# Output projection of the pooling chunks as seven products of quartered matrices, with the sums of quarters made two stages earlier and kept in DRAM

## Chip, cores, metric

The kernel runs on one core of a Trainium2 chip. The metric is the device time of one execution in microseconds, the median of several runs. TensorE (PE) multiplies, VectorE (DVE), ScalarE (ACT) and GpSimd (POOL) do the elementwise work, and SyncE (SP) issues most of the DMAs.

## What is computed

One layer of a streaming encoder on x of 1024 rows by 1024 columns, in float32:

```python
h = rmsnorm(x, norm1_g)
proj = h @ w_in                      # q, k, v (512 each), 8 forget logits, u (512)
attn = forgetting_attention(q, k, v, log_f)       # 8 heads of 64, causal
pool = multiscale_pool(u, w_pool, pool_scale)     # 4 groups of 128 channels
mixed = concat([attn, pool])         # 1024 rows x 1024
x = x + mixed @ w_out                # the output projection
h2 = rmsnorm(x, norm2_g)
x = x + (silu(h2 @ w_gate) * (h2 @ w_up)) @ w_down
y = rmsnorm(x, final_g)
```

The change concerns the line `x + mixed @ w_out`. Its contraction of 1024 is cut into eight chunks of 128: chunks 0 to 3 are the four pairs of attention heads, chunks 4 to 7 the four pooling groups.

## The kernel before

Every large product is made in three matmuls of a reduced-precision type. `split` (L119) copies a page to a high part on ACT (L120) and subtracts it from the page on DVE or POOL for a low part (L121). `mm3` (L159) multiplies high by high, high by low and low by high (L161 to L163).

The input projection and the pooling groups come first; the four pooled chunks are stored to the DRAM tensor `mixd`. Then `attend` (L711) runs four times, once for each pair of heads. A pair has eight jobs (two heads by four blocks of 256 rows). A job's steps are the turning of probabilities (`turn`, L634), the products with the values (`values`, L651, into the single bank `po`), `combine` (L662), which stores the attention rows to `mixd` through SP, and the `scores` (L605) of the next job: matmuls, a masked minimum on DVE, an exponential on ACT, a reciprocal on DVE and a normalisation on POOL (L629). Scores run one job ahead (`LOOK = 1`).

Between these steps `attend` takes matmuls from a generator, the filler; `counts` says how many filler steps each job is given. For the first three pairs the filler is the projection of the next pair's q and k (`project`, L533), and the values of the last two pairs (`project_v23`, L580). The order of the trace of the program gives priorities; a planner then fixes each engine's order by its own estimate of when operands are ready, so a filler matmul may come earlier than its place in the text. On each engine, and in the DMA queue of SP, the order is then fixed.

In the last pair the filler is the first part of the output projection. `first_rows` (L817) multiplies chunks 4 and 5 for the eight row tiles, `second_rows` (L844) chunks 6, 7 and 0. A row tile has two halves of 512 columns; each half is one accumulation in one of the two PSUM banks with the tag "m" (`rows2`, L803), then a DVE add into the row of x2 in SBUF (L811). There are 32 filler steps; 27 are given to the jobs, one is taken behind them, and four are held behind the last product with the values (`mark["pv"]`, L897). Then `last_row` (L873) adds chunks 1, 2 and 3 to each row, stores it and goes on to the second norm and the gate and up projections. The chunk of the last pair, mix 3, comes back from DRAM in two halves (`mix_halves`, L859).

A page of 128 by 1024 is loaded by `raw_page` (L750) into a raw tile and split by `split_page` (L756). Raw tiles have the tag "wr" with two buffers, which also holds the raw weights and the low half of the keys in `project`; some raw pages are loaded to tiles of the pool `outp`, which opens with `xw` (the rows of x2) when the transposed input `hTh`, `hTl` is freed behind the last projection. `first_chunk` (L763) splits chunk 4 during the third pair. The buffer "vc" of `vpool` holds `pf01` at first, and then the values of the third pair.

Of the kernel before, what the change touches and what calls it, by code (L numbers as in the profile page):

```python
# [8 lines left out]
F32 = mybir.dt.float32  # L9
# [6 lines left out]
P = 128  # L16
S = 1024
# [28 lines left out]
def tile_kernel(  # L46
# [664 lines left out]
    def attend(p, fill, counts, drain=True):  # L711
# [7 lines left out]
        for n in range(2 * NSB):  # L719
            steps = job_steps(2 * NSB * p + n)  # L720
# [23 lines left out]
    attend(0, project(1), [5, 4, 4, 3, 8, 6, 6, 0])  # L744
    attend(1, both(project(2), project_v23()), [10, 7, 6, 8, 10, 8, 12, 0])
    W, VB, VC = (wpool,), (vpool, ("vb",), 1), (vpool, ("vc",), 1)
    ST0, ST1 = (ap_, ("st0", "st0"), 6), (ap_, ("st1", "st1"), 6)
    raw_pages = {}

    def raw_page(kind, c, pl, tag):  # L750

        t = raw_pages[kind, c] = pl.tile([P, 1024], F32, tag=tag, bufs=2, name=f"r_{kind}{c}")
        row = (PAIR[c] if c < NPAIR else c) * P
        nc.sync.dma_start(out=t, in_=mixd[c] if kind == "mix" else w_out[0, row : row + P, :])

    def split_page(kind, c, to, eng):  # L756
        pages = page_tiles(to, f"{kind}{c}")
        split(*pages, raw_pages.pop((kind, c)), eng)
        return pages

    ahead = {}

    def first_chunk():  # L763

        for kind, to in (("mix", VB), ("wo", W)):
            raw_page(kind, NPAIR, wpool, "wr")
            ahead[kind] = [split_page(kind, NPAIR, to, nc.gpsimd)]
        raw_page("mix", NPAIR + 1, wpool, "wr")
# [46 lines left out]
    last = {}  # L815

    def first_rows():  # L817

        raw_page("wo", 5, op, "ol")
        x2_load(ORDER[0])  # L820
        lhs, rhs = ahead["mix"], ahead["wo"]
        lhs.append(split_page("mix", 5, M, nc.vector))
        rhs.append(split_page("wo", 5, O, nc.vector))
        x2_load(ORDER[1])
        for kind, c, tag in (("wo", 6, "oh"), ("mix", 6, "ml"), ("wo", 7, "mh"), ("mix", 7, "ol")):
            raw_page(kind, c, op, tag)
        later = [
            ("wo", 6, VC, nc.vector), ("mix", 6, ST0, nc.gpsimd), ("wo", 7, W, nc.vector),
            ("mix", 7, ST1, nc.gpsimd), ("wo", 0, ST0, nc.vector), ("mix", 0, VB, nc.gpsimd),
        ]  # L830
        for n, tt in enumerate(ORDER):
            if n + 2 < NT:
                x2_load(ORDER[n + 2])
            if n == 2:
                raw_page("wo", 0, wpool, "wr")
# [594 lines left out]
```

## Time and profile before

| | before |
|---|---|
| median of 3 runs | 1035.35 us (1035.22 to 1036.37) |
| profiled execution: span from first to last instruction | 1033.6 us |
| profiled execution: its own time | given by its span alone |
| PE, DVE, ACT, POOL busy | 1024.3, 632.8, 454.2, 381.1 us |
| mean granted TensorE clock | 0.998 |
| HBM read, written | 86.29 MB, 33.03 MB |

The profile is one execution. Busy time is the time in which at least one instruction of the engine was recorded; matmuls are pipelined, so a record of a matmul is longer than the distance to the next. A releaser behind an idle time is the operation that ended it, inferred from semaphores. A window row gives a stretch, then for PE, weight loads, DVE, ACT and POOL the busy time and the number of instructions, then the granted clock, the share of the DMA engines and GB/s; for one tile it lists only the engines that touch the tile.

### The profile page before, as it was taken

To read this page: it belongs to the slowest core of one execution; us is meant where nothing else is said; L and a number is where in the kernel's file an instruction comes from. 1 tells how busy PE (TensorE), PEld (TensorE's weight loads), DVE (VectorE), ACT (ScalarE), POOL (GpSimd) and SP (SyncE) were. 2 spreads that over 40 slices of the span, in tenths; PEclk is the share of its full clock that TensorE was granted. 3 is DMA by queue.
4 is the path that set the end of the run, shared out by engine and by line. 5 is a ranking of instruction groups with operands and counts; after the bars stand their busy time and mean duration, and the time that the engine had idled before them with its cause. 6 is when DMAs were issued, how large, how long until landed. Compare 5 with 4: busy or idle time off the path is not lost.

```text
span 1033.6 us, 14202 instructions
## 1 busy us (share of the span) xinstructions
PE 1024.3 (99%) x5104; PEld 868.9 (84%) x5104; DVE 632.8 (61%) x1000; ACT 454.2 (44%) x733; POOL 381.1 (37%) x312
## 2 busy tenths in 40 slices
PE   9999999999999999999999999999999999999997
PEld 7988888998888888888888888888888888888886
DVE  7565566776886479744433334334334789788886
ACT  7434355665665257533333233233233343333346
POOL 4350121213346043447537536636637510000045
PEclk9999999999999999999999999999999999999999
DMA  7224434333643134343143143143236755353424
GB/s 251 53 47 143 105 81 103 84 102 89 224 175 106 49 136 129 103 143 112 62 132 113 62 133 112 64 131 113 81 113 251 248 204 175 110 198 97 153 92 163
DMA packets 108439, 130.21 MB, mean 126 GB/s; under 512 B 7369, under 2 KB 70353, under 8 KB 108369
## 3 DMA queue, kind: packets, MB, share of 16 engines
q1 hardware_dynamic: 96544, 108.18, 33.4%
q10 hardware_dynamic: 11504, 20.47, 5.2%
q8 instruction: 40, 0.66, 0.2%
q0 software_dynamic: 320, 0.66, 0.2%
q14 instruction: 31, 0.25, 0.1%
HBM read 86.29 MB, written 33.03 MB: 115 GB/s over the span
## 4 chain that ended last, share of the span: by engine, by line
PE 98%; DMA 1%; ACT 0%; DVE 0%; POOL 0%; issue 0%; ACTq 0%; POOLq 0%
PE gu_P L161 14%; PE gu_P L162 14%; PE gu_P L163 14%; PE d L161 7%; PE d L162 7%; PE d L163 7%; PE po L657 4%; PE tp L643 3%; PE o L161 3%; PE o L162 3%; PE qk L161 3%; PE qk L162 3%; PE qk L163 3%; PE o L163 3%; PE v L374 2%; PE z L618 2%
## 5 line engine op out<-in xcount | busy, mean ns | idle before, releaser
L121 DVE TENSOR_TENSOR gu_P_l<-s,gu_P_h 128x1024 fp32r<-128x1024 f32 (+1 forms) x48 | 66.5, 1393 | 98.6 <-ACT gu_P_h L120 98.5
L162 PE MATMUL d<-d,d 128*128 128x512 f32 (+1 forms) x308 | 119.5, 388 | 0.0
L163 PE MATMUL d<-d,d 128*128 128x512 f32 (+1 forms) x308 | 119.5, 388 | 0.0
L629 POOL TENSOR_SCALAR p<-p,rr 128x128 f32<-128x128 f32 (+3 forms) x64 | 48.6, 764 | 175.5 <-DVE rr L628 140.2
L161 PE MATMUL d<-d,d 128*128 128x512 f32 x308 | 107.8, 388 | 0.0
L120 ACT ACTIVATE d<-r_f 128x1536 fp32r<-128x1536 f32 (+1 forms) x28 | 38.8, 1384 | 117.6 <-PE d L162 101.6
L121 DVE TENSOR_TENSOR gu_P_l<-r,gu_P_h 128x1024 fp32r<-128x1024 f32 x32 | 48.9, 1527 | 64.3 <-ACT gu_P_h L120 64.3
L1063 POOL TENSOR_TENSOR s<-r 128x1024 f32<-128x1024 f32 x10 | 24.0, 2401 | 161.9 <-DMA r<-in_w_up_dram 116.0
L120 ACT ACTIVATE gu_P_h<-r 128x1024 fp32r<-128x1024 f32 x32 | 33.8, 1060 | 91.1 <-PE gu_P L162 35.5
L162 PEld LDWEIGHTS d<-d,d 128*128 128x128 f32 x308 | 57.8, 188 | 12.0 <-DVE d L121 0.2
L161 PEld LDWEIGHTS d<-d,d 128*128 128x128 f32 x308 | 57.8, 188 | 12.0
L163 PEld LDWEIGHTS d<-d,d 128*128 128x128 f32 x308 | 57.8, 188 | 11.9
L626 ACT ACTIVATE p<-p,mn 128x128 f32<-128x128 f32 (+3 forms) x64 | 49.3, 772 | 32.8 <-DVE mn L620 29.9
L1291 POOL TENSOR_SCALAR sse<-sse 128x1 f32<-128x1 f32 x7 | 3.5, 494 | 158.1 <-ACT junk L1287 158.1
L1150 POOL TENSOR_TENSOR h<-h,qh 128x512 f32<-128x512 f32 x33 | 44.3, 1345 | 32.3 <-ACT qh L1148 24.1
L648 DVE TENSOR_TENSOR tl<-tp,th 128x512 fp32r<-128x512 f32 (+1 forms) x80 | 49.3, 632 | 10.7 <-ACT th L647 9.7
L120 ACT ACTIVATE gu_P_h<-s 128x1024 fp32r<-128x1024 f32 (+1 forms) x48 | 47.0, 984 | 19.7 <-PE gu_P L162 13.0
L1147 DVE TENSOR_TENSOR qh<-gu_P,sn_sU 128x512 f32<-128x512 f32 x22 | 15.2, 690 | 60.5 <-POOL h L1150 43.2
L121 DVE TENSOR_TENSOR d<-r_f,d 128x1536 fp32r<-128x1536 f32 (+1 forms) x28 | 45.7, 1633 | 10.5 <-ACT d L120 10.5
L163 PE MATMUL qk<-hTh,l_qk 128*128 128x512 f32 x128 | 50.7, 396 | 0.0
L161 PE MATMUL qk<-hTh,h_qk 128*128 128x512 f32 x128 | 50.6, 395 | 0.0
L162 PE MATMUL qk<-hTl,h_qk 128*128 128x512 f32 x128 | 50.4, 394 | 0.0
(337 smaller groups left out, 3067.1 us busy)
## 6 DMA issues: line engine op xcount, KB each, us to landing
r_f<-hsdP SPq DMA_DIRECT2D x77, 256.0 KB
r_wd<-in_w_down_dram SPq DMA_DIRECT2D x22, 512.0 KB
hsdP<-f ACTq DMA_DIRECT2D x43, 256.0 KB
r<-in_w_gate_dram SPq DMA_DIRECT2D x21, 512.0 KB
r<-in_w_up_dram SPq DMA_DIRECT2D x21, 512.0 KB
s<-hi SPq DMA_DIRECT2D x64, 128.0 KB
hsdP<-h ACTq DMA_DIRECT2D x32, 256.0 KB
x<-in_x_dram SPq DMA_DIRECT2D x8, 512.0 KB
```

Of the source, the lines that this page charges most:

```text
L120: mark["hi"] = nc.scalar.activation(out=hi, in_=src, func=AF.Copy)
L121: return eng.tensor_tensor(out=lo, in0=src, in1=f32(hi), op=ALU.subtract)
L161: nc.tensor.matmul(ps, lh, rh, start=start, stop=False, **kw)
L162: nc.tensor.matmul(ps, lh, rl, start=False, stop=False, **kw)
L163: mark["mm"] = nc.tensor.matmul(ps, ll, rh, start=False, stop=stop, **kw)
L626: nc.scalar.activation(out=pr[:, :n], in_=pr[:, :n], func=AF.Exp, scale=-1.0, bias=mn, accum_out=rs)
L629: nc.gpsimd.tensor_scalar(out=pr[:, :n], in0=pr[:, :n], scalar1=rr, scalar2=1.0, op0=ALU.mult, op1=ALU.mult)
L643: nc.tensor.transpose(tp[:, w : w + P], probs[h, 2 * sb + a][:, s * P : (s + 1) * P], ident)
L648: nc.vector.tensor_tensor(out=tl[:, :w], in0=tp[:, :w], in1=f32(th[:, :w]), op=ALU.subtract)
L657: mark["pv"] = nc.tensor.matmul(po[:, first * P : 2 * P], vt[p][:, s, j, :], part[:, o : o + wd], start=(s == 0 and part is th), stop=(s = ...
L1063: g(out=s1, in0=a21, in1=a22, op=ALU.add)
L1150: nc.gpsimd.tensor_tensor(out=h, in0=h, in1=q, op=ALU.mult)
```

## The change

The four pooling chunks are taken as one product of a 1024 x 512 matrix by a 512 x 1024 matrix, cut into quarters of 512 x 256 and 256 x 512, and computed by the Winograd form of Strassen's method: seven products of quarters in place of eight, and eight sums of quarters, four for each side.

- `quarter_load`, `quarter_sums` and `quarter_store` make these sums in four rounds during the first two pairs of heads. A round loads four half pages (two DMAs of 512 KB) into one tile of 1 MB with the tag "vc", makes four sums in place on POOL and stores the tile to a DRAM tensor `sumd`. The twelve parts are put in at the beginnings of jobs by the new argument `events`.
- `raw_page` loads an operand of a product in two halves of 256 KB, from `mixd` and `w_out` or from `sumd`, always into a "wr" tile. `SPLITS` lists the pages with the engine of the low part and the filler step before which each is put; each loads the page two places on.
- The filler is one generator, `output_steps`, of 32 steps. P6 goes to four halves of two new tiles `total` (an ACT copy). P7 is added to x2, and its bank is then continued with P4. P1 is added to the totals, and POOL adds them to x2; its bank is continued with P2 and chunk 0. P5 is added to the totals, which POOL adds to two places of x2. P3 takes chunk 0 in the same bank. The last four steps, `rest`, are chunk 0 for the remaining eight half rows, one bank for each three matmuls.
- The loads of the eight rows of x2, put in one for each row before, are all put in ahead of the last pair.
- Chunks 1, 2 and 3 are split as before, through the list, and multiplied in `last_row` as before.

The core of the diff:

```diff
+    def quarter_load(r):
+        kind, i = rounds[r]
+        t = quarters[r] = vpool.tile([P, 4, 512], F32, tag="vc", bufs=1, name=f"quarters{r}")
+        for k in range(2):
+            dst = t[:, 2 * k : 2 * k + 2, :].rearrange("p a e -> p (a e)")
+            nc.sync.dma_start(out=dst, in_=page_source(kind, NPAIR + 2 * k + i))
...
+        if rounds[r][0] == "mix":
+            go(q3, q1, q3, ALU.add)
+            go(q1, q0, q1)
+            go(q0, q3, q0)
+            go(q2, q2, q0)
...
+    def quarter_store(r):
+        nc.sync.dma_start(out=sumd[rounds[r]], in_=quarters[r])
...
+    attend(0, project(1), [5, 4, 4, 3, 8, 6, 6, 0], events={n: side(n) for n in range(8)})
+    attend(
+        1, both(project(2), project_v23()), [10, 7, 6, 8, 10, 8, 12, 0], events={n: side(8 + n) for n in range(4)}
+    )
...
+        t = raw_pages[kind, c] = wpool.tile([P, 1024], F32, tag="wr", bufs=2, name=f"r_{kind}{c}")
...
+    def add_total(c, *places):
+        for tt, hf in places:
+            out = x2_half(tt, hf)
+            nc.gpsimd.tensor_tensor(out=out, in0=out, in1=total_of(c), op=ALU.add)
+
+    def part(ps, k, c, start, stop):
+        (ah, al), (bh, bl) = operands["mix", k], operands["wo", k]
+        for i in range(2):
+            ts, hs = slice(i * 512 + c * P, i * 512 + (c + 1) * P), slice(i * 512, (i + 1) * 512)
+            mm3(ps, ah[:, ts], al[:, ts], bh[:, hs], bl[:, hs], start and i == 0, stop and i == 1, True)
...
+    SPLITS = [
+        ("mix", "P7", M, nc.vector, -1), ("wo", "P7", O, nc.vector, 0),
+        ("mix", "P4", M, nc.vector, 2), ("wo", "P4", O, nc.vector, 3),
+        ("mix", "P1", VB, nc.gpsimd, 4), ("wo", "P1", W, nc.gpsimd, 5), ("wo", "P2", W, nc.gpsimd, 6),
+        ("mix", 0, VC, nc.gpsimd, 7), ("wo", 0, ST1, nc.vector, 8), ("mix", "P2", O, nc.vector, 11),
+        ("mix", "P5", M, nc.gpsimd, 12), ("wo", "P5", O, nc.gpsimd, 13), ("wo", 1, M, nc.gpsimd, 14),
+        ("mix", "P3", VB, nc.vector, 19), ("wo", "P3", W, nc.vector, 20), ("wo", 3, W, nc.gpsimd, 21),
+        ("mix", 1, O, nc.gpsimd, 22), ("mix", 2, M, nc.gpsimd, 25), ("wo", 2, O, nc.gpsimd, 26),
+    ]
...
+        order = [(p6, c) for c in range(NH)] + pairs(p7, p4) + pairs(p1, p2)
+        order += [(f, c) for f in (p5, p3, rest) for c in range(NH)]
+        for s, (f, c) in enumerate(order):
+            ahead_of(s)
+            f(c)
+            yield
+
+    raw_page(*SPLITS[1][:2])
+    ahead_of(-1)
+    for tt in (*range(NH, NT), *range(NH)):
+        x2_load(tt)
+    fill = output_steps()
     attend(3, fill, [3, 3, 4, 4, 4, 4, 3, 2], drain=False)
```

More of the change, by code (lines that the diff above doesn't have):

```diff
@@ L747, in tile_kernel @@
     ST0, ST1 = (ap_, ("st0", "st0"), 6), (ap_, ("st1", "st1"), 6)
[L748 to L754, printed above, removed]
+    raw_pages, operands = {}, {}
+    QUARTER = dict(
+        mix=dict(P1=(0, 0), P2=(1, 0), P4=(1, 1), P6=0, P7=1, P3=2, P5=3),
+        wo=dict(P1=(0, 0), P2=(1, 0), P3=(1, 1), P5=0, P7=1, P4=2, P6=3),
+    )
@@ L842, in tile_kernel @@
[L842 to L853 removed]
+    total = [ap_.tile([P, S], F32, tag="st0", bufs=6, name=f"total{n}") for n in range(2)]
```

137 lines of the change are left out of this document (94 added, 43 removed).

## The prediction

> **What bounds the kernel now.** I read the first part of the page, then the chain that ended last, then the waits of PE, then the busy times of the one stage that the change rebuilds.
>
> ```profile
> span 1033.6 us, 14202 instructions
> PE 1024.3 (99%) x5104; PEld 868.9 (84%) x5104; DVE 632.8 (61%) x1000; ACT 454.2 (44%) x733; POOL 381.1 (37%) x312
> PE 98%; DMA 1%; ACT 0%; DVE 0%; POOL 0%; issue 0%; ACTq 0%; POOLq 0%
> ...
> 264.80:349.80 85.00, 85.00 (x506) 74.97 (x505) 64.44 (x156) 48.88 (x94) 34.86 (x27) 1.00 0.45 154
> 349.80:358.20 8.40, 8.40 (x40) 6.98 (x39) 3.71 (x6) 1.64 (x3) 0.00 (x0) 1.00 0.24 73
> ...
> PE warm L254 <- DVE junk L252: 1.2, 1, 1.2
> ...
> PE spread L264 <- DVE gcol L260: 0.3, 1, 0.3
> ```
>
> TensorE is busy in 99% of the span and is 98% of the chain. Its listed waits are four, of 2.5 us in sum, all in the opening. The two window rows are the last pair of heads (264.8 to 349.8 us), where the first part of the output projection is the filler between attention steps, and the stretch after the last attention product. Columns: length, PE, PEld, DVE, ACT, POOL busy, granted clock, DMA share, GB/s. PE has no gap in either, DVE is busy for 64.44 of 85.00 us. So a product taken away is worth its PE time, as long as the rest of the filler is ready when PE wants it.
>
> **The change, part by part.**
>
> *Products removed.* Before, the filler is 16 output blocks (8 row tiles by 2 halves) of five chunks, three matmuls each: 240. After it is seven products of 4 row tiles, 2 contraction halves and 3 matmuls (168) plus chunk 0 for 16 blocks (48): 216. The last three chunks stay. So 24 matmuls go. Their price is not the 0.39 us of a record, since they are pipelined, but the distance between starts:
>
> ```profile
> 350.25 0.39 PE L162 MATMUL o<-hl_wo,h_mix 128*128 128x512 f32 x1
> ...
> 357.99 0.39 PE L163 MATMUL o<-h_wo,hl_mix 128*128 128x512 f32 x1
> 358.21 0.39 PE L161 MATMUL o<-h_wo,h_mix 128*128 128x512 f32 x1
> ...
> 349.97:358.21 8.24, 8.24 (x36) 6.81 (x37) 2.06 (x3) 1.00 0.25 75
> 358.41 0.69 DVE L811 TENSOR_TENSOR x_s<-o,x_s 128x512 f32<-128x512 f32 x1 [0.63 <-PE o L163]
> ```
>
> The last row of the window counts 36 from 349.97, so 35 from 350.25 to 358.21: 7.96 / 35 = 0.2274 us. 24 x 0.2274 = 5.46 us, 0.53% of the span. Twelve of them leave the stage with attention (204 to 192), twelve the tail behind the last attention product (36 to 24).
>
> *The last four steps are two-bank bound.* Each of the eight last blocks ("rest") has three matmuls in one of two banks, then a DVE add. Above, the third matmul starts at 357.99 and its add ends at 358.41 + 0.69 = 359.10, 1.11 us later. A bank is then busy 2 x 0.2274 + 1.11 = 1.56 us, and with 0.05 us for PE to restart 1.61; PE needs 6 x 0.2274 = 1.36 for two blocks. Lost: 0.25 us per pair, four pairs: **+1.0 us**. Below: 0, if something else fills. Above: two splits of mix chunk 3 push in front of the adds:
>
> ```profile
> 353.84 0.69 DVE L121 TENSOR_TENSOR mix_l<-r_mix,mix_h 128x512 fp32r<-128x512 f32 x1 [0.86 <-ACT mix_h L120]
> 356.49 0.69 DVE L121 TENSOR_TENSOR mix_l<-r_mix,mix_h 128x512 fp32r<-128x512 f32 x1 [1.35 <-ACT mix_h L120]
> 359.57 0.39 PE L161 MATMUL o<-h_wo,mix_h 128*128 128x512 f32 x1
> ```
>
> 2 x 0.6 more makes 2.2 us. The tail also covers the trip of mix chunk 3 through DRAM: its first half is ready at 354.53, wanted at 359.57, and with 12 x 0.2274 = 2.7 us less at 356.8. 2.3 us of slack stay; no cost. The second half (357.18) is wanted a row later, nearly 4 us on.
>
> *Pages.*
>
> ```profile
> L647 ACT ACTIVATE th<-tp 128x512 fp32r<-128x512 f32 x18 | 10.3, 592 | 0.9
> ...
> 268.21 1.07 ACT L120 ACTIVATE h_wo<-r_wo 128x1024 fp32r<-128x1024 f32 x1 [0.96 <-DMA r_wo<-in_w_out_dram]
> 266.04 1.22 DVE L121 TENSOR_TENSOR l_mix<-r_mix,h_mix 128x1024 fp32r<-128x1024 f32 x1
> ```
>
> Before, the filler and its successor need 15 split pages, after 21 (fourteen quartered pages, two of chunk 0, five of the last chunks). Each is a load, an ACT copy of 1.06 us (a bank copy, as in the first row, takes 0.59) and a subtraction. In the stage with attention ACT gets six more copies and four bank copies of 0.6: 48.9 + 8.8 = 57.7 us; DVE three splits more and four adds fewer: 64.4 + 3.7 - 2.7 = 65.4; the stage is 85.0 - 2.7 = 82.3 us long, so neither becomes the bound by its sum. What changes is the supply: before, five raw pages go to tiles of the new pool at once; after, all go through the two "wr" slots (three of them before this stage), the load of one waiting for the split two places ahead. What such a slot delivers stands in the trace:
>
> ```profile
> 308.09 0.33 SPq L754 DMA_DIRECT2D r_mix<-mixd  x1
> ...
> 312.49 0.33 SPq L754 DMA_DIRECT2D r_wo<-in_w_out_dram  x1
> 315.26 0.33 SPq L754 DMA_DIRECT2D r_mix<-mixd  x1
> ...
> 319.52 0.33 SPq L754 DMA_DIRECT2D r_wo<-in_w_out_dram  x1
> 312.84 2.39 POOL L121 TENSOR_TENSOR l_mix<-r_mix,h_mix 128x1024 fp32r<-128x1024 f32 x1 [0.38 <-ACT h_mix L120]
> ```
>
> One slot: 308.09 to 315.26 and 312.49 to 319.52, 7.1 us with a POOL split; with DVE's 1.22 for 2.40, 5.9. The first pages have a worse start:
>
> ```profile
> 263.84 0.34 SPq L754 DMA_DIRECT2D r_wo<-in_w_out_dram  x1
> 264.27 0.38 SPq L795 DMA_DIRECT2D x_r<-in_x_dram  x1
> 278.92 0.46 SPq L573 DMA_DIRECT2D s<-lo  x1
> 264.80:276.00 11.20, 11.20 (x67) 9.91 (x66) 10.46 (x29) 7.87 (x14) 1.92 (x2) 1.00 0.98 346
> 264.80:275.70 10.90, 6.31 (x24) 4.35 (x24) 1.27 (x2) 1.00 0.98 345
> 264.80:283.10 18.30, 9.86 (x38) 6.88 (x39) 3.90 (x6) 1.00 0.92 301
> 264.80:289.00 24.20, 12.77 (x48) 8.80 (x49) 5.32 (x8) 1.00 0.92 317
> 264.80:309.00 44.20, 25.72 (x95) 17.00 (x96) 10.08 (x15) 1.00 0.66 227
> ```
>
> Weight page P7 can't be loaded before the split of mix page P7 has freed its slot (266.04 + 1.22 = 267.26; the other slot holds the low half of the keys until the store of 278.92 has landed). From 263.9 on nothing holds back the eight loads of x2 rows, 0.52 MB each; at the 346 GB/s of that stretch 1.5 us apiece. If none is ahead, the page lands 4.4 us after its issue (as 263.84 to 268.21, where ACT had waited for it), is split by 274.0, and PE, which has 24 matmuls of P6 to do and by the fourth-last row did 24 by 275.7, loses nothing. If all eight are ahead it lands at 264.3 + 12.1 + 4.4 = 280.8 and is split by 283.1; PE had done 38 by then, so 14 are missing: 3.2 us. Behind it the slots pass a page per 7.1 or 5.9 us each: page P4 by about 289 (cap 36, before 48), the ninth of the list, mix P2, by about 309 (cap 84, before 95). These gaps don't add up; the largest, 3.2 us, is the end of the range. Six loads ahead, the likeliest by SP's rate of issue, make about 11 missing matmuls, 2.5 us. PE doesn't stand still for all of that: of the 18.3 us to 283.1 it spent 38 x 0.2274 = 8.6 on the filler, and attention, which had the other half, can move up. I take half: **+1.2 us**; ends 0 and 3.2.
>
> *POOL.* Added: four rounds of four sums in the first two pairs and twelve adds of totals in the last, each 128x512; three splits more.
>
> ```profile
> L1150 POOL TENSOR_TENSOR h<-h,qh 128x512 f32<-128x512 f32 x33 | 44.3, 1345 | 32.3 <-ACT qh L1148 24.1 <-ACT d L120 8.3
> L629 POOL TENSOR_SCALAR p<-p,rr 128x128 f32<-128x128 f32 (+7 forms) x31 | 22.7, 736 | 114.3 <-DVE rr L628 95.7 <-PE z L618 9.4 <-PE z L617 6.5
> 188.82 0.26 ACT L206 ACTIVATE v<-v 128x128 fp32r<-128x128 f32 x1
> 333.24 1.13 POOL L629 TENSOR_SCALAR p<-p,rr 128x1024 f32<-128x1024 f32 x1 [6.59 <-DVE rr L628]
> 342.89 1.28 PE L643 MATMUL tp<-ident,p 128*128 128x128 f32 x10
> 315.00:350.00 35.00, 35.00 (x206) 30.71 (x205) 21.23 (x43) 14.39 (x27) 11.19 (x8) 1.00 0.17 58
> ```
>
> Sums: 16 x 1.345 = 21.5 us beside 22.7 busy us in the 102 us of the first pairs (second row). Each round blocks a normalisation by up to 4 x 1.345 = 5.4 us; PE covers it with projection matmuls that are ready. The round's tile must be free for the values of the third pair, first written at 188.82. A round is load 2 x 1.5 + 2.9, sums 5.4, store the same 5.9: 17.2; four from 112.6 end at 181.4. 7.4 us spare, cost nil; a delay beyond that would halt the value products, at about half of PE's time. In the last pair POOL goes to 34.9 + 12 x 1.345 + 3 x 2.4 = 58.2 of 82.3 us: not a bound by the sum.
>
> *SP.* 12 issues for the rounds, 28 instead of 8 for the pooling pages: 32 x 0.35 = 11 us over three stages, on a queue mostly waiting. Stores of attention rows and of stacks stand behind them; their cover is the one job by which scores run ahead; without it PE would wait up to 11 us in all, which no row suggests.
>
> **Sum.** -5.46 + 1.0 + 1.2 = -3.3 us against the profiled execution's span of 1033.6. The median of the runs, 1035.35, is 1.75 us above that span; I add the same: **1032.1 us**.
>
> **Rivals.** A difference within 0.2% (2.1 us) can't be told from none here.
>
> 1. Everything is covered, and both stalls vanish: 1035.35 - 5.46 = 1029.9. For it: PE's records show no wait after the opening, though ACT waited for the raw page at 268.21. Against: the two-bank arithmetic. Chance 0.20.
> 2. Supply starves the filler in full: -5.46 + 3.2 + 2.2 gives 1035.3, the change moves matmuls into idle time and does nothing. For it: the two slots and 346 GB/s at 98% DMA share. Against: attention can move up. From 1033.3 to 1037.4, 0.22.
> 3. Slower: POOL's in-order queue takes over as the bound of the last two jobs. The four P5 steps put eight adds (10.8 us) there, with two splits (4.8) beside them. Ahead of the last normalisation (333.24, wanted by the turn at 342.89, 8.5 us after its end) these 15.6 us would hold PE for 7.1, and the time is 1032.1 + 7.1 = 1039.2; it decides from a hold of 5.3 us. Against: POOL is idle for 24 of the 35 us around it now (last row above), and the adds arrive spread over four steps. Chance 0.13.
> 4. A gap of PE in one piece costs more than itself, if matmuls behind it run at a lower clock; the granted clock is 1.00 in every row above, so no row prices that. Bounded by the nearest, 0 and one gap's length again (3.2 us on rival 2, 1038.5). Chance 0.02.
>
> [...]
>
> **Chances.** Forecast (1030.9 to 1033.3) 0.43; rivals 0.20, 0.22, 0.13, 0.02. Faster 0.63, same 0.22, slower 0.15. The range runs from the full gain, 1029.7 with the runs' spread, through the stalls' upper ends (1035.3) into a hold of POOL of about 4.5 us, 1036.6; beyond lie under 2 in 10.
>
> **What would show it.** After: PE instructions down by 24 from 5104; the start distance still 0.227; tail of 24 matmuls some 6.5 us long rather than 5.5; PE waits (or gaps) between 275 and 290 us for P7 and P4; POOL near 58 us in the stage; the values' first write still near 189. The prediction is wrong if PE waits for a normalisation, if that first write moves out, or if the gaps before 290 exceed 3 us.

## The result, and the profile after

The changed kernel takes 1046.28 us (median of 4 runs, 1044.37 to 1047.20) beside 1035.38 us for the kernel before on the same chip: ratio 1.0098, 95% interval 1.0083 to 1.0112. It is slower by 10.9 us, where the prediction had 3.3 us less, and 9.7 us above the range's upper end. The profiled execution has a span of 1044.1 us against 1033.6, so the traces hold 10.5 us of it.

The first part of the page of the changed kernel, and its chain that ended last:

```profile
span 1044.1 us, 14280 instructions
PE 1025.3 (98%) x5080; PEld 865.3 (83%) x5080; DVE 637.8 (61%) x1003; ACT 462.5 (44%) x743; POOL 424.2 (41%) x343
...
PE 86%; DMA 5%; ACT 3%; DVE 2%; POOL 1%; issue 1%; SPq 1%; ACTq 0%; POOLq 0%; DVEq 0%
```

5080 matmuls are the 24 fewer that were to go, and yet PE is busy 1 us longer. A record of 0.39 us reaches beyond the 0.2274 us to the next start, so a gap of up to 0.16 us doesn't show as idle time; and records at a lower clock are longer (0.63 us for a 128x512 matmul from 315.51 on, where the granted clock is 0.50, and 0.39 to 0.40 again from 319.08 on). The chain shows what happened: it was 98% PE, now 11% of the span runs through DMA, ACT, DVE and POOL. PE waits where it never did.

Where, is told by cutting the span at three starts: the last q/k matmul, the first matmul of `last_row`, and the last matmul of `last_row`. The windows are cut at these starts (columns as in the prediction), first for the kernel before:

```profile
263.64:358.21 94.57, 94.57 (x549) 83.05 (x548) 68.89 (x163) 51.25 (x98) 34.86 (x27) 1.00 0.43 146
358.21:395.99 37.78, 37.78 (x192) 31.81 (x191) 29.64 (x39) 22.65 (x41) 19.80 (x23) 1.00 0.40 139
```

and for the changed one, with the tail alone in the last row:

```profile
265.36:365.24 99.88, 93.67 (x526) 79.58 (x524) 73.69 (x166) 59.52 (x108) 57.97 (x42) 0.98 0.52 169
365.24:406.19 40.95, 38.83 (x193) 31.74 (x191) 30.04 (x39) 22.32 (x41) 19.21 (x23) 1.00 0.37 129
356.63:365.24 8.61, 6.82 (x28) 4.36 (x27) 6.19 (x10) 1.64 (x3) 0.63 (x1) 1.00 0.22 71
```

| stretch | before | after | difference |
|---|---|---|---|
| start to last q/k matmul (opening, first three pairs) | 263.64 | 265.36 | +1.72 |
| to the first matmul of `last_row` (last pair and tail) | 94.57 | 99.88 | +5.31, where -5.46 was to come from the matmuls |
| to the last matmul of `last_row` | 37.78 | 40.95 | +3.17 |
| to the end | 637.6 | 637.9 | +0.3 |

The middle stretch has thus lost 5.31 + 5.46 = 10.8 us beside its gain. 99.88 - 93.67 = 6.2 us of it are idle time of PE. The longest waits of PE in it:

```profile
PE o L161 <- ACT h_woP L120: 1.3, 1, 1.3
PE o L161 <- DVE x_s L876: 1.1, 1, 1.1
PE tp L643 <- DVE tl L648: 1.0, 1, 1.0
PE o L162 <- DVE l_woP L121: 0.8, 1, 0.8
PE o L161 <- ACT h_mixP L120: 0.7, 1, 0.7
```

`h_woP`, `l_woP` and `h_mixP` are pages of the new list; `x_s` from line 876 is an add that must free a bank; `tl` belongs to attention itself. How a late page reaches attention is seen around one of them, in the timeline of SP, DVE, ACT and PE of the changed kernel:

```profile
310.31 0.80 SPq L809 DMA_DIRECT2D r_mixP<-mixd  x2
310.56 1.26 DVE L121 TENSOR_TENSOR l_wo<-r_wo,h_wo 128x1024 fp32r<-128x1024 f32 x1 [0.77 <-ACT h_wo L120]
312.34 1.27 DVE L648 TENSOR_TENSOR tl<-tp,th 128x512 fp32r<-128x512 f32 x2
313.16 1.23 PE L643 MATMUL tp<-ident,p 128*128 128x128 f32 x7 [0.98 <-DVE tl L648]
313.98 1.06 ACT L120 ACTIVATE h_mixP<-r_mixP 128x1024 fp32r<-128x1024 f32 x1 [1.38 <-DMA r_mixP<-mixd]
315.06 0.98 ACT L647 ACTIVATE th<-tp 128x384 fp32r<-128x384 f32 x2
315.09 0.62 PE L161 MATMUL o<-h_woP,h_mixP 128*128 128x512 f32 x1 [0.70 <-ACT h_mixP L120]
```

Raw page P2 is asked for at 310.31, when its slot comes free. ACT, whose order is fixed, stands at the copy of this page until 313.98 with nothing to do for 1.38 us; attention's own copy `th` is behind it and starts at 315.06. DVE had the subtraction of another page (`l_wo`, weight chunk 0) in front of `tl`. So PE has neither a product nor an attention step. What follows costs as much again:

```profile
312.00:315.09 3.09, 1.33 (x10) 0.77 (x8) 2.36 (x7) 1.46 (x3) 3.09 (x4) 1.00 0.80 266
315.09:319.08 3.99, 3.99 (x15) 3.60 (x16) 3.42 (x7) 2.93 (x5) 2.18 (x2) 0.57 0.51 138
```

1.76 us idle in 3.09, then 3.99 us at a mean granted clock of 0.57: 0.43 x 3.99 = 1.7 us more. The signs that the prediction named for being wrong don't show this loss: PE waits for no normalisation in this stage, PE's idle time from the last q/k matmul to 290 us is 1.2 us and not over 3, and the values' first write (190.49) is 1.7 us later, as late as the whole run is by then.

### The profile page after: what moved, and what is told of

Its sections match the earlier page's. It is cut to its first block, busy times and chain, and to the rows that moved or that the text cites. A ratio compares the mean times of both kernels' runs of the same rounds, so it can differ in the third digit from the quotient of the medians.

```text
span 1044.1 us, 14280 instructions
## 1 busy us (share of the span) xinstructions
PE 1025.3 (98%) x5080; PEld 865.3 (83%) x5080; DVE 637.8 (61%) x1003; ACT 462.5 (44%) x743; POOL 424.2 (41%) x343
## 4 chain that ended last, share of the span: by engine, by line
PE 86%; DMA 5%; ACT 3%; DVE 2%; POOL 1%; issue 1%; SPq 1%; ACTq 0%; POOLq 0%; DVEq 0%
PE gu_P L162 13%; PE gu_P L161 13%; PE gu_P L163 13%; PE d L161 7%; PE d L162 7%; PE d L163 7%; PE po L657 3%; PE tp L643 2%; PE qk L163 2%; PE qk L161 2%; PE qk L162 2%; PE v L374 2%; PE u L161 1%; PE u L163 1%; PE u L162 1%
## 5 line engine op out<-in xcount | busy, mean ns | idle before, releaser
L120 ACT ACTIVATE gu_P_h<-s 128x1024 fp32r<-128x1024 f32 (+1 forms) x48 | 47.0, 984 | 20.7 <-PE gu_P L162 14.9
```

Source lines behind the costliest of these rows:

```text
L120: mark["hi"] = nc.scalar.activation(out=hi, in_=src, func=AF.Copy)
```

## The experiments

Every run is compared with the kernel before on its own chip. The three stretches are taken from one profile each, as above; the last q/k matmul alone spreads by some 2 us over kernels with the same rounds (264.77 to 266.98), so a difference below 1 us in a single row means little. One kernel's executions spread as well: the four of mix0_vb from 1043.25 to 1052.65 us, those of rest_first from 1041.97 to 1048.53, while the kernel before keeps within 2.1 us on each chip. So the medians say what a change is worth, and a profile says where one execution lost its time.

| run | median us | ratio to before, 95% | last q/k | to `last_row` | `last_row` |
|---|---|---|---|---|---|
| changed kernel | 1046.28 | 1.0098 (1.0083 to 1.0112) | 265.36 | 99.88 | 40.95 |
| before_rounds | 1037.59 | 1.0017 (1.0008 to 1.0027) | 265.04 | 96.20 | 37.78 |
| no_rounds | 1042.95 | 1.0066 (1.0051 to 1.0081) | 263.44 | 99.63 | 39.83 |
| no_pages | 1039.60 | 1.0036 (1.0024 to 1.0049) | 265.77 | 93.29 | 40.35 |
| resident | 1043.54 | 1.0079 (1.0059 to 1.0100) | 264.77 | 100.90 | 41.10 |
| resident2 | 1039.78 | 1.0042 (1.0027 to 1.0057) | 265.98 | 94.09 | 40.78 |
| slots_vc | 1045.93 | 1.0099 (1.0082 to 1.0116) | 265.56 | 99.72 | 40.94 |
| slots_x2 | 1047.42 | 1.0109 (1.0087 to 1.0131) | 266.04 | 102.53 | 40.68 |
| rest_first | 1047.09 | 1.0099 (1.0072 to 1.0127) | 266.98 | 99.84 | 41.14 |
| mixl_pool | 1043.64 | 1.0076 (1.0061 to 1.0091) | 266.15 | 98.87 | 39.82 |
| mix0_vb | 1047.22 | 1.0113 (1.0078 to 1.0149) | 265.95 | 103.83 | 37.86 |
| rounds_later | 1045.27 | 1.0096 (1.0081 to 1.0111) | 265.37 | 100.44 | 39.44 |
| fix_all | 1048.07 | 1.0117 (1.0093 to 1.0140) | 265.28 | 105.95 | 38.50 |
| cand | 1044.53 | 1.0079 (1.0062 to 1.0095) | 266.20 | 100.69 | 37.91 |
| closure | 1036.67 | 1.0005 (0.9996 to 1.0015) | 263.34 | 94.20 | 38.15 |

**The rounds: before_rounds, no_rounds, rounds_later.** The first adds `quarter_load`, `quarter_sums`, `quarter_store` and the events to the kernel before.

> The kernel before with the four quarter rounds added (loads, 16 sums on POOL, stores to DRAM) and nothing that reads them. Theory R (the rounds cost time where they stand: the last q/k projection matmul came 1.7 us later after the change): 1035.4 + 1.7 = 1037.1 us, the last qk matmul near 265.4 us instead of 263.6, and every later stage as long as before. Rival (the rounds lie beside PE for nothing and the 1.7 us come from another order of the early matmuls): within 0.5 us of before. If the rounds also disturb the last pair, the stretch from the last qk matmul to the last value product would grow beyond 86.2 us.

The rounds alone cost 2.05 us; the last q/k matmul comes 1.4 us later. The stretch behind it is longer too (96.20 against 94.57) in this profile, with no work added there. One place suggests how a round costs PE time. In SP's order the transfers of the next pair's stacks (`augd` is the first) stand behind the last store of a round. In before_rounds:

```profile
158.45 0.33 SPq L779 DMA_DIRECT2D sumd_mix<-quarters  x1
159.16 0.27 SPq L549 DMA_DIRECT2D s<-augd  x1
```

The transfer of `augd` is issued 2.7 us later than in the kernel before (156.43), and up to 166.70 PE waits 0.89 us for a bank of the q/k projection. The changed kernel has the same wait (0.89 us up to 167.02); the kernel before and no_rounds have none. That the late stacks cause this wait is my reading; no run takes the store alone away. The second run takes the rounds out of the changed kernel:

```diff
-    attend(0, project(1), [5, 4, 4, 3, 8, 6, 6, 0], events={n: side(n) for n in range(8)})
+    attend(0, project(1), [5, 4, 4, 3, 8, 6, 6, 0])
...
-                src = sumd[kind, i][:, at, :]
+                src = page_source(kind, NPAIR + 2 * (at // 2) + i)[:, (at % 2) * 512 : (at % 2 + 1) * 512]
```

> The changed kernel without the four rounds: pages of sums are loaded from the unsummed quarters at the same places with the same number of DMAs (the sums are left out of the products). The rounds alone cost 2.05 us in the kernel before, 1.4 of it up to the last q/k matmul. If that holds here too, 1046.3 falls by 1.4 to 2.1 to 1044.2 to 1044.9, the last q/k matmul comes near 263.9 us, and the later stages keep their lengths. Rival (the rounds also disturb the last pair, by the state in which they leave the queues): more than 3 us.

The last q/k matmul is at 263.44, as before the change, and 3.3 us go in all: the rounds' share is shown from both sides, 2.05 added and about 3 taken away. The 3.3 us lie above the 1.4 to 2.1 expected and just above the rival's 3; 1.9 us of them come before the last q/k matmul, and whether the rounds disturb the later stages too is left open by this spread. The third puts them two jobs later:

```diff
-    attend(0, project(1), [5, 4, 4, 3, 8, 6, 6, 0], events={n: side(n) for n in range(8)})
+    attend(0, project(1), [5, 4, 4, 3, 8, 6, 6, 0], events={n: side(n - 2) for n in range(2, 8)})
...
```

> The changed kernel with each of the twelve parts of the rounds put two jobs later (jobs 2 to 7 of the first pair, 0 to 5 of the second). Theory R1 (the 1.2 us by the first scores matmul come from the loads that SP issues ahead of the stacks): first z near 112.6 instead of 113.8, last qk at 264 to 264.4, time 1046.3 - 1.0 to 1.5 = about 1045. Rival R2 (POOL's sums of 1.29 us in front of normalisations): nothing gained, the loss moves to a later job.

This told nothing of R1 and R2. The planner left the loads where they were, so the rounds weren't moved: the first two are issued at the same time as in the changed kernel. First the row of rounds_later, then that of the changed kernel:

```profile
96.08 0.83 SPq L759 DMA_DIRECT2D quarters<-in_w_out_dram  x2
```

```profile
96.04 0.83 SPq L759 DMA_DIRECT2D quarters<-in_w_out_dram  x2
```

**The pages: no_pages, resident, resident2.**

```diff
+    for kind in ("mix", "wo"):
+        for k in ("P1", "P2", "P3", "P4", "P5", "P7"):
+            operands[kind, k] = operands[kind, "P6"]
+    SPLITS = [e for e in SPLITS if not isinstance(e[1], str)]
...
```

> The changed kernel, where the six quartered products after P6 multiply P6's operand pages again: their twelve pages are neither loaded nor split (this part of the result is left out on purpose of timing; all matmuls, adds and the whole pages stay). Theories S (two raw slots) and Q (the queues of ACT, DVE and POOL are held by the splits) both say that the stretch from the last q/k matmul to the first matmul of last_row falls from 99.9 us to 91 to 93 (89.1 is PE's own work there), the time from 1046.3 to about 1038. If the loss lies in the adds, the banks or attention itself, it stays above 97.

99.88 falls to 93.29: the twelve pages cost 6.6 us (6.7 by the medians). The stretch falls into the part with attention, up to the last product with the values, and the tail. First the part with attention of the kernel before, then both parts of no_pages:

```profile
263.64:349.85 86.21, 86.21 (x512) 76.12 (x511) 65.19 (x157) 49.61 (x95) 34.86 (x27) 1.00 0.45 153
```

```profile
265.77:350.46 84.69, 84.04 (x500) 73.99 (x499) 59.50 (x149) 46.18 (x93) 44.19 (x37) 1.00 0.36 118
350.46:359.06 8.60, 6.79 (x28) 4.36 (x27) 6.19 (x10) 1.64 (x3) 0.00 (x0) 1.00 0.22 71
```

The tail lost twelve matmuls and takes 8.60 us, before 8.36; it is treated below. The part with attention lost twelve, too, and is 1.5 us shorter, not 12 x 0.2274 = 2.7. The missing 1.2 us lie in its last job. The last filler matmul that may run there starts at 344.82, the last turn at 346.42, and its sixteen products with the values follow at once and wait for the copies, twice for a third of a microsecond; the first time here:

```profile
347.79 0.39 PE L657 MATMUL po<-th,v 128*128 128x256 f32 x1 [0.31 <-ACT th L647]
```

Before the change 18 filler matmuls stood between this turn and its products, and PE waited for nothing. The other two runs keep the splits and take away only what comes before them, resident for the quartered pages, resident2 for mix 0 and weight 0 as well:

```diff
+        if isinstance(c, str) and c != "P6":
+            raw_pages[kind, c] = f32(vt[3].rearrange("p s j d -> p (s j d)")[:, 0:1024])
+            return
...
```

> The changed kernel, where those twelve pages are split as before, each on its engine and at its place, but from a tile that lies in SBUF (the values of the last pair) instead of from loaded raw pages: no load and no slot stands between two splits (the sums are left out of the products). Theory S: as without pages, the stretch falls to 91 to 94 us, 1038 to 1041. Theory Q: the splits still stand in the queues, so the stretch stays at 97 to 100 us, 1044 to 1046.

The stretch was 100.90, against theory S on its face. The profiled execution is the slowest of the four (1046.71 us; two others took 1042.2). The timeline of ACT and PE shows one event behind it:

```profile
290.37 1.06 ACT L120 ACTIVATE h_wo<-r_wo 128x1024 fp32r<-128x1024 f32 x1 [6.72 <-DMA r_wo<-in_w_out_dram]
291.33 1.07 ACT L647 ACTIVATE th<-tp 128x512 fp32r<-128x512 f32 x2
293.33 0.90 PE L643 MATMUL tp<-ident,p 128*128 128x128 f32 x3 [4.08 <-DVE tl L648]
```

The page of weight chunk 0 was still loaded, and the planner had put its copy early. ACT waited 6.72 us for that one transfer, attention's `th` stood behind it, and PE had 4.1 us of nothing. The windows of the gap and of what followed:

```profile
289.00:293.33 4.33, 0.25 (x2) 0.00 (x0) 1.88 (x3) 2.92 (x5) 0.00 (x0) 0.89 0.16 63
293.33:297.00 3.67, 3.67 (x11) 2.88 (x12) 2.77 (x7) 1.87 (x3) 2.38 (x1) 0.50 0.51 165
```

The other executions have a higher mean clock (0.997 to 0.999, this one 0.994), so this event need not be in them.

> As the run with split pages from a resident tile, which had one gap of 4.1 us and a half clock behind it where a raw page of the weight chunk 0 was late and stood first in ACT's order; now the two pages of chunk 0 too are split from the resident tile, so that only the five last whole pages are loaded (the sums and chunk 0 are left out of the products). Theory S (late raw pages): no gap before 340 us, clock 1.00, the stretch from the last q/k matmul to last_row 92 to 95 us, time 1038 to 1040.5. Theory Q (the splits' own time in the queues): the stretch stays at 97 or more, time above 1042.

With these two pages resident as well, the stretch is 94.09 and the clock 1.00 in it:

```profile
265.98:360.07 94.09, 91.43 (x526) 78.45 (x525) 74.91 (x166) 58.41 (x108) 56.04 (x42) 1.00 0.32 102
```

All splits are in the queues (DVE 74.91 us, POOL 56.04; 73.69 and 57.97 in the changed kernel), and 5.8 of the 6.6 us are gone, by the medians 6.5 of 6.7. So the engines have room for the splits; the raw pages come too late for the order that is fixed on ACT. Theory S holds; theory Q is worth under 1 us here, with two pages less to load than in no_pages.

**More slots: slots_vc, slots_x2.** Both keep the result and give the early pages other raw tiles.

```diff
+    both_raw = vpool.tile([P, 2, 1024], F32, tag="vc", bufs=1, name="r_vc")
+    spare["wo", "P7"], spare["mix", "P4"] = both_raw[:, 0, :], both_raw[:, 1, :]
...
```

> The changed kernel, with the raw pages of weight P7 and mix P4 in the buffer vc, which is empty until the split of mix 0; the two wr slots then begin with weight P4 and mix P1, two list places earlier than before. Theory S (the two raw slots starve the filler of the last pair): PE's idle 2.5 us between 276 and 293 and its idle 1.8 us with the half clock (1.6 us more) between 311 and 322 shrink; the stretch from last qk to last value product falls from 91.2 us to 86 to 88, the time from 1046.3 to 1041 to 1043. If it is only the order in which x2 rows are loaded ahead of P7, the first gap stays. Rival (DVE, ACT or POOL queues with more splits hold PE, whatever the slots): the stretch stays within 1 us of 91.2.

I had taken `vc` for empty; it isn't until the third pair's last values are read. The page was issued at 293.61, where the changed kernel has 269.85:

```profile
293.61 1.78 SPq L813 DMA_DIRECT2D r_vc<-sumd_wo  x2
298.74 1.06 ACT L120 ACTIVATE h_woP<-r_vc 128x1024 fp32r<-128x1024 f32 x1 [1.50 <-DMA r_vc<-sumd_wo]
```

The filler stood at 24 matmuls from 277.5 to 299.8, the attention ran ahead, and the stretch came out the same, 99.72. So attention did fill most of a page's absence of 22 us, though not all of it: PE was idle for 3.6 us between 280 and 300, against 1.9 in the changed kernel. The products put off then stood in the tail, 66 matmuls in 17.96 us, which is 2.9 us above their 66 x 0.2274.

```diff
+    spare["wo", "P7"], spare["mix", "P4"] = (xw_tile(t, f"raw_{t}")[:, 0, :] for t in ("s1", "s3"))
...
+            if s in (5, 6):
+                x2_load(s - 3)
...
```

> The changed kernel with the raw pages of weight P7 and mix P4 in the tiles of two rows of x2 (rows 2 and 3, wanted only by the fifteenth filler step; their loads come later), so that three pages are loaded ahead of the x2 rows and no page waits for the low half of the keys. All is computed as in the changed kernel. Theory S: the idle times between 275 and 293 us go (2.5 us), the caps move up by one or two pages, so the gap at 311 to 316 and the half clock behind it (3.4 us) shrink too: stretch 94 to 97, time 1040.5 to 1043.5. If instead the page rate of the two slots later on decides, the first gaps go and others come: stretch above 98.5.

The first pages did come ahead of the x2 rows, and the stretch grew to 102.53, the expectation's other case. The planner had moved the copies up as well, and new gaps came; in one, PE waits 2.4 us for a subtraction on DVE that took 3.36 us beside one on POOL, as in fix_all below.

**Tail and rows: rest_first, mixl_pool, mix0_vb.**

```diff
-        order += [(f, c) for f in (p5, p3, rest) for c in range(NH)]
+        order += [(f, c) for f in (p5, rest, p3) for c in range(NH)]
```

> The changed kernel with the last twelve filler steps in the order P5, rest, P3: the blocks of nine matmuls come last, and twelve matmuls move from the stage with attention to the tail. Theory B (the three-matmul blocks are bound by two banks and their adds in the tail): the tail takes 36 x 0.2274 = 8.2 us plus under 1, the stage with attention 2.7 us less, unless the same waits appear there; the sum of both falls from 91.2 + 8.6 by 2 to 3 us, 1046.3 to about 1043.8. Rival (the waits follow the rest blocks into the stage, or the second half of mix 3 is what is late): sum unchanged.

The sum did not move (99.84). The tail did as theory B says: 42 matmuls, six of them of the last `rest` blocks, in 10.38 us, 0.8 above their 42 x 0.2274 where the changed kernel loses 3.15. The part with attention took it back, and not by waits of the small blocks that moved there: from 340 us to its last product PE is idle for 1.7 us, where it was busy throughout in the changed kernel, and 1.31 of them are one wait for a `th` (at 354.36), in front of which ACT stood for 2.31 us at the copy of weight 2. It is once more a late page. So theory B is borne out for the tail and not for the sum.

```diff
-            split(hi[:, hs], lo[:, hs], raw[:, hs])
+            split(hi[:, hs], lo[:, hs], raw[:, hs], nc.gpsimd)
```

> The changed kernel with the low halves of mix chunk 3 made on POOL, which is idle in the tail (0.56 us busy of 8.54), not on DVE, where each stands in front of adds that free the two banks. Theory B2 (in the tail the adds wait behind the subtraction of mix 3, which waits for its trip through DRAM: 0.7 to 0.9 us twice): the tail falls from 8.6 us to about 7.3, the time from 1046.3 to about 1045. Rival B (two banks and the adds alone, 6.4 us and more): the tail stays above 8.2 us.

In the changed kernel the second subtraction of mix 3 waits for its half page's trip through DRAM, and an add that frees a bank is behind it on DVE:

```profile
362.42 0.63 ACT L120 ACTIVATE mix_h<-r_mix 128x512 fp32r<-128x512 f32 x1 [2.20 <-DMA r_mix<-mixd]
363.09 0.69 DVE L121 TENSOR_TENSOR mix_l<-r_mix,mix_h 128x512 fp32r<-128x512 f32 x1 [0.89 <-ACT mix_h L120]
363.70 1.28 DVE L876 TENSOR_TENSOR x_s<-o,x_s 128x512 f32<-128x512 f32 x2
```

With these two subtractions on POOL the window of the tail is

```profile
357.84:365.02 7.18, 6.70 (x27) 4.10 (x26) 5.17 (x8) 1.64 (x3) 1.79 (x2) 1.00 0.26 86
```

7.18 us instead of 8.61, as theory B2 said; closure, with the same edit, has 7.17. 7.18 - 5.46 = 1.7 us are left for the two banks. PE begins a pair of blocks at 359.77, 361.52, 363.27 and 365.02, so each takes 1.75 us, where six matmuls need 1.36.

```diff
-        ("mix", "P1", VB, nc.gpsimd, 4), ("wo", "P1", W, nc.gpsimd, 5), ("wo", "P2", W, nc.gpsimd, 6),
-        ("mix", 0, VC, nc.gpsimd, 7), ("wo", 0, ST1, nc.vector, 8), ("mix", "P2", O, nc.vector, 11),
+        ("mix", "P1", VC, nc.gpsimd, 4), ("wo", "P1", W, nc.gpsimd, 5), ("wo", "P2", W, nc.gpsimd, 6),
+        ("mix", 0, VB, nc.gpsimd, 7), ("wo", 0, ST1, nc.vector, 8), ("mix", "P2", O, nc.vector, 11),
...
-        ("mix", "P3", VB, nc.vector, 19), ("wo", "P3", W, nc.vector, 20), ("wo", 3, W, nc.gpsimd, 21),
+        ("mix", "P3", VC, nc.vector, 19), ("wo", "P3", W, nc.vector, 20), ("wo", 3, W, nc.gpsimd, 21),
```

> The changed kernel with buffers exchanged: the page mix 0 goes to vb, mix P1 and mix P3 to vc, so vc is free for the raw gate and up page after the last P3 step, not after the last rest step. Theory V (the raw page of gate and up that waits for vc comes 1.4 us later relative to the rows, its POOL split then stands ahead of a norm's scale, and the adds of rows behind that): the stretch from the first last_row matmul to the last one of the rows falls from 44.2 us to about 41, the time from 1046.3 to about 1043; the raw page is issued some 5 us earlier. Rival (the longer stretch comes from the rows' own pages, mix 1, mix 2 and weight 2, split later): the stretch stays near 44.

The rows fall to 37.86, what they were before the change; in the three other runs in which that raw page comes early they take 37.91 to 38.50, in all other runs of the changed kernel 39.4 to 41.1. Theory V is shown. In the changed kernel the raw page of gate and up is issued 0.2 us after the first matmul of `last_row` (before the change 1.2 us ahead), ACT and POOL take it up among the rows, and the norm's scale stands behind its split:

```profile
365.43 0.38 SPq L1115 DMA_DIRECT2D r_gu_P<-in_w_gate_dram  x1
369.08 1.06 ACT L120 ACTIVATE gu_P_h<-r_gu_P 128x1024 fp32r<-128x1024 f32 x1 [6.02 <-DMA r_gu_P<-in_w_up_dram]
370.21 2.41 POOL L121 TENSOR_TENSOR gu_P_l<-r_gu_P,gu_P_h 128x1024 fp32r<-128x1024 f32 x1 [12.95 <-ACT gu_P_h L120]
372.71 0.19 POOL L125 TENSOR_SCALAR ms_b<-ss_b 128x1 f32<-128x1 f32 x1
```

But the time did not fall, because the stretch before grew to 103.83. Attention had run ahead (its last product is at 351.46), and POOL's row of adds and splits stood in the tail. DVE could not begin the first `mix_l` until POOL had read a tile; then the two of them, 0.69 us each in the changed kernel, took 3.44 us, while POOL split the page of gate and up that this very edit had brought forward. An add was behind them, and PE waited 3.5 us:

```profile
359.55 2.39 POOL L121 TENSOR_TENSOR l_wo<-r_wo,h_wo 128x1024 fp32r<-128x1024 f32 x1
361.97 3.44 DVE L121 TENSOR_TENSOR mix_l<-r_mix,mix_h 128x512 fp32r<-128x512 f32 x2 [0.45 <-POOL l_wo L121]
362.53 2.34 POOL L121 TENSOR_TENSOR gu_P_l<-r_gu_P,gu_P_h 128x1024 fp32r<-128x1024 f32 x1 [0.59 <-ACT gu_P_h L120]
366.07 0.50 PE L161 MATMUL o<-h_wo,hl_mix 128*128 128x512 f32 x1 [3.53 <-DVE x_r L876]
```

That is near rival 3 of the prediction, POOL's queue as the bound, in a neighbour of the kernel it was written for; but what it held is an add, not a normalisation.

**All cures: fix_all, cand.** fix_all joins slots_x2, mixl_pool, mix0_vb and rounds_later, with the low halves of mix 2 and weight 2 on DVE; cand leaves out the slots and the rounds. Their only edit not shown yet:

```diff
-        ("mix", 1, O, nc.gpsimd, 22), ("mix", 2, M, nc.gpsimd, 25), ("wo", 2, O, nc.gpsimd, 26),
+        ("mix", 1, O, nc.gpsimd, 22), ("mix", 2, M, nc.vector, 25), ("wo", 2, O, nc.vector, 26),
```

> All cures together, the same result as the changed kernel: the two raw pages in rows of x2, the low halves of mix 3 on POOL, mix 0 in vb and mix P1 and P3 in vc, the rounds two jobs later, and the low halves of mix 2 and weight 2 on DVE, so that POOL's row of adds at the end is shorter. Sum of the single terms if they add up: 1046.3 - 4 (slots) - 1.4 (tail, as mixl_pool showed) - 3.1 (rows, as mix0_vb showed) - 1.2 (rounds) = 1036.6, the kernel before within 0.2%. If terms overlap, 1038 to 1041. Below 1035.4 only if the stage with attention comes to 92 us or less.

> The same result as the changed kernel, with the three cures that cost nothing elsewhere: low halves of mix 3 on POOL, mix 0 in vb and mix P1 and P3 in vc, and the low halves of mix 2 and weight 2 on DVE, so that the tiles of mix 3 are freed earlier. If the tail's 1.4 and the rows' 3.1 us add up: 1046.3 - 4.5 = 1041.8. If the pages' waits move with every other order of the queues, the stretch with attention takes some of it back: 1043 to 1046. Either way above the kernel before (1035.4).

fix_all missed all of its values (1048.07 us); cand, at 1044.53, lies in the second of its two ranges, in which the pages' waits move. The rows' gain stayed (38.50, 37.91) and the stretch with attention took it back (105.95, 100.69). As I read it, each change of a buffer or an engine makes another order, and the pages are late for that one too. In fix_all the longest gap comes from two splits that meet:

```profile
315.01 4.16 DVE L121 TENSOR_TENSOR l_wo<-r_wo,h_wo 128x1024 fp32r<-128x1024 f32 x1
```

```profile
314.50 2.37 POOL L121 TENSOR_TENSOR hl_mix<-r_mix,hl_mix 128x1024 fp32r<-128x1024 f32 x1
316.81 1.27 POOL L889 TENSOR_TENSOR x_r<-x_r,total 128x512 f32<-128x512 f32 x1
```

**The account: closure.** No rounds, no twelve pages, `mix_l` on POOL, and the raw page of gate and up in `vb`:

```diff
-    pages[0, "P1"] = gu_page("gu0_P1", src, raw="vc")
+    pages[0, "P1"] = gu_page("gu0_P1", src, raw="vb")
...
```

> All four costs that the runs so far have priced taken out at once: no rounds, no loads and splits for the twelve quartered pages after P6 (their products use P6's pages again), the low halves of mix 3 on POOL, and the raw page of gate and up in vb, which is free after the P3 steps. What stays of the change is its matmuls, adds and whole pages (the sums and the other quarters are left out of the products). If the account is complete and the 24 matmuls are worth 5.46 us: stretch from the last q/k matmul to last_row 91 to 92 us (94.57 - 5.46 + two banks' 1.0 to 1.7), rows as before (37.8), time 1031 to 1033. If the matmuls taken away are worth less than that in this stage, or a cost has been missed (POOL's adds of the totals, say): 1035 or more.

1036.67 us, no different from the kernel before, and above the 1031 to 1033 of a complete account. The early stretch (263.34) and nearly the rows (38.15) are back, and still the middle one is 94.20 where 94.57 - 5.46 plus 1.7 for the banks would be 90.8. The missing 3.4 us lie in the part with attention, most of them in its last job. A window of it, and the timeline of ACT and PE:

```profile
345.00:350.00 5.00, 3.17 (x20) 2.26 (x18) 2.85 (x5) 3.31 (x6) 2.17 (x1) 1.00 0.25 72
```

```profile
346.69 1.06 ACT L120 ACTIVATE gu_P_h<-r_gu_P 128x1024 fp32r<-128x1024 f32 x1 [0.65 <-DMA r_gu_P<-in_w_up_dram]
347.65 1.45 ACT L647 ACTIVATE th<-tp 128x512 fp32r<-128x512 f32 x3
348.29 0.38 PE L657 MATMUL po<-th,v 128*128 128x256 f32 x1 [0.84 <-ACT th L647]
```

As in no_pages, all filler that may run ahead of the last product is used up (at 343.4), and the last job's sixteen products wait for the copies of their own turn. And here the copy of the gate and up page, which my edit brought forward into this job, waits for its transfer in front of three `th`. From the last turn to the last product PE has the same instructions in both runs; they take 344.72 to 350.37, 5.65 us, against 346.42 to 350.46, 4.04 us, in no_pages. So 1.6 of the missing 3.4 us are this run's own, about 1.2 are the missing filler, as in no_pages, and some 0.6 are not assigned to anything. By subtraction, an estimate, the kernel without those 1.6 would take 1035.1 us, 0.6 below the kernel before on this chip: with all priced costs gone, little of the 5.46 us would be left.

## Why the prediction was wrong, point by point

- **What bounds the kernel.** Right: PE, with no gaps. But "a product taken away is worth its PE time, as long as the rest of the filler is ready" had a second condition that I did not see. The filler is also the cover for attention's own latency. In no_pages, with every quartered page ready, the part with attention fell by 1.5 us where 2.7 were to come, because its last job had no filler left. Whether another division of the filler over the jobs (`counts`) would avoid this, no run shows.
- **Products removed, -5.46.** The count was right (5104 to 5080), and the price holds for PE's own work. The stage paid 1.5 of 2.7 us for the twelve matmuls of the part with attention, and nothing for the twelve of the tail (next point).
- **Last four steps, +1.0 (0 to 2.2).** Measured 8.61 - 5.46 = 3.15, above the upper end. The two banks are 1.7: a pair of blocks takes 1.75 us in mixl_pool, not 1.61, since the first matmul behind a wait stands 0.34 us ahead of the next (361.52, then 361.86), not 0.23; the 0.05 us to restart PE came out as 0.06 (in the changed kernel adds end at 360.25 and 361.60, PE starts at 360.31 and 361.66). The other 1.4 are the subtractions of mix 3 in front of the adds. I had them as the upper end, 2 x 0.6, and left them out of the sum; and the second was late as well, by the trip through DRAM, for which I said "no cost". PE did not want that half page yet, but its subtraction stands in DVE's order in front of adds that PE wants. I asked who uses the page, not what queues behind its split.
- **Pages, +1.2 (0 to 3.2).** Measured 6.6: this is the step that failed most. The supply of the first page went as worked out, that of the later ones was slower: weight P7 was split by 278.9 (between 274.0 and 283.1), P4 by 293.5 (forecast 289), mix P2 by 316.5 (forecast 309). Two sentences failed. "Attention can move up" does not hold when attention's copies stand behind the late page on ACT. And "these gaps don't add up" is wrong: each page that ACT meets too early is a stop of its own (PE's waits for `l_woP`, `h_woP` and `h_mixP` above end at 278.94, 292.25 and 315.09, at P7, P4 and P2). The half clock behind one gap, 1.7 us, is part of the 6.6; it is rival 4, with a chance of 0.02, and it needed no 3.2 us in one piece: the longest idle time ahead of the fall was 0.98 us.
- **Quarter rounds, nil.** Their end was forecast late (the last store is issued at 158.3, forecast 181.4), and the values' tile was not delayed by them. The cost is 2.05 us all the same. "PE covers it" failed. How the 1.4 us before the last q/k matmul arise is not settled, since the rounds could not be moved. A wait of 0.89 us near 167 us, which the kernel before and no_rounds don't have, points at the order that the *SP* paragraph names, stacks behind the stores of rounds, and at a cover that it took to be enough.
- **POOL, 58.2 us.** Measured 57.97, and not the bound: resident2 keeps all its splits and adds, 56.04 us, and has 94.09. Its order became one as soon as attention ran ahead (mix0_vb).
- **Not in the sum.** The rows of `last_row`, +3.2 us: the diff puts mix 0 into `vc` up to the last step, and I followed that buffer backwards (third pair's values) but not forwards, to the page that waits for it.

Rounds 1.7, pages 6.6, tail 3.15, rows 3.2 and 0.3 make 14.9; less 5.46 that is 9.5 of the 10.5 us; the missing 1.0 is about what the last job without filler costs in no_pages (1.2). Of the rivals, number 2 named the right place, but took a starved filler to cost at most what the change gains.

## What to carry to other kernels

When the orders of all engines are fixed, price a late transfer by what stands behind its first reader on that reader's engine, not by whether the consumer has other work. Matmuls that fill the gaps of a chain with latency can be worth less than their own time when they are taken away; look at what the chain would wait for without them. And follow each buffer that a change occupies longer to the next tile that waits for it.

## What the runs showed of the hardware

In the changed kernel the granted clock fell to half after 3.09 us in which PE was busy for 1.33, with no single idle time over 0.98 us. In closure, 1.8 us idle within 5 left it at 1.00. In the changed kernel's trace the clock is full for 310.61 us, half for 3.41 and full for 723.63, which are 91, 1 and 212 times 3.413; in the trace of the kernel before it is full for 1024.00, 300 times 3.413. So I cut the traces into windows of 3.41 us, counted from these changes. In the sixteen traces the clock fell nine times before the programs' ends (twice in mix0_vb, once each in the changed kernel, resident, mixl_pool, slots_x2, rounds_later, fix_all and cand), and in the window ahead of each fall PE was busy for 0.3 to 1.94 of 3.41 us. The window of the changed kernel with the one behind it, and that of cand:

```profile
311.91:315.32 3.41, 1.65 (x11) 1.09 (x11) 2.68 (x7) 1.69 (x3) 3.41 (x4) 1.00 0.83 274
315.32:318.73 3.41, 3.41 (x14) 3.02 (x14) 3.19 (x7) 2.70 (x5) 1.60 (x2) 0.50 0.40 98
```

```profile
278.28:281.69 3.41, 1.94 (x9) 1.14 (x8) 2.37 (x7) 3.36 (x6) 0.00 (x0) 1.00 1.03 420
```

Two windows with no more work in them kept the clock: one of slots_x2 from 315.97, with PE busy for 1.73 us, and one at the end of the changed kernel, with the window behind it:

```profile
1035.53:1038.94 3.41, 1.66 (x14) 1.45 (x13) 2.78 (x6) 2.93 (x9) 2.15 (x5) 1.00 0.87 334
1038.94:1042.36 3.42, 0.00 (x0) 0.00 (x0) 0.75 (x1) 0.72 (x1) 0.41 (x1) 1.00 0.81 310
```

So a fall needed neither one long idle time nor a window without work, and PE's busy time in the window ahead does not by itself tell the falls from the rest. What decides is not shown.

A DVE subtraction of a page, 1.22 us in the changed kernel (267.76), took 4.16 us in fix_all. It started at 315.01, while POOL worked from 314.50 to 318.08 on two operations, and ended at 319.17, 1.1 us after them. The one of slots_x2, 3.36 us, ran from 316.68 to 320.04 beside a POOL split from 316.60 to 318.96, and also ended 1.1 us after it. As this is near the 1.22 us of the subtraction alone, I read both as held and not slowed; no run tests it. In the changed kernel's last pair and tail the longest such split took 1.76 us, so little of its loss is from this; in mix0_vb it is 2.1 of the 3.44 us above.
